# Moving the modulation tiles of a two-layer decoder to other places in the instruction stream

## The chip, the cores and the metric

The kernel runs on one core of one Trainium2 chip. The metric is the device time of one execution in microseconds (us). Three runs of the kernel before gave 2732.73 us as their median (2731.3 to 2734.19).

## The reference

The computation is a trunk of two decoder layers over 1024 tokens of width 1024. A vector `c` modulates each layer: six vectors of 1024 are made from it and used as shift, scale and gate.

```
c_act = silu(c)
for l in range(2):
    mod = c_act @ w_ada[l] + b_ada[l]                 # 6 * 1024 values
    sh1, sc1, g1, sh2, sc2, g2 = split(mod, 6)
    h = rms_norm(x, ln1_g[l]) * (1 + sc1) + sh1
    z = h @ w_in[l]            # pool input, q and kv latents, rope key, two gates
    y_a = pool_mixer(...) @ p_pool[l]
    y_b = causal_attention(...) @ p_attn[l]
    merged = sigmoid(gz_a) * y_a + sigmoid(gz_b) * y_b
    x = x + g1 * (merged @ w_out[l])
    h2 = rms_norm(x, ln2_g[l]) * (1 + sc2) + sh2
    x = x + g2 * (relu(h2 @ w_ff1[l]) ** 2 @ w_ff2[l])
return rms_norm(x, final_g)
```

All arrays are float32. The order of the six vectors matters here: a tile is 128 outputs of `w_ada`, so tiles 0 to 7 of a layer are sh1, 8 to 15 sc1, 16 to 23 g1, 24 to 31 sh2, 32 to 39 sc2 and 40 to 47 g2.

## The kernel before

Every product is made of three matmuls of TensorE on fp32r operands (high times high, high times low, low times high), so that each operand needs a split: a cast on ScalarE (line 305, or 254 for weights) and a subtraction on VectorE (line 306, or 256 for weights; GpSimd makes the latter for a few weights). `x` and `h` are kept transposed, 128 features by 512 tokens a tile, with two token halves `c`.

A layer runs in this order. The latent projections, the pool mixer, and q, k and v with stores to DRAM. Then the gate blocks, a loop `m` from 0 to 7: for `m` under `NA` = 4 a gate block of the input projection (48 matmuls) and the pool projection (24), for the others the pool projection alone; at `m` = 6 `attention_open` (line 1290) takes buffers and loads the first head. Then the attention, a score and a value stage for each head and token half, with the remaining 12 gate blocks (`fill`) as filler on TensorE. Then the attention's projection with the merge, the output projection (8 blocks `m` by two halves, 24 matmuls each; head and tail of three blocks run half by half), in whose tail the second norm of each half is made. Last the channel mixing in eight groups: groups 0 to 6 (`seven`) have an f1 stretch of four blocks (192 matmuls at line 292) and a product stretch (168 matmuls at line 1235, seven products in place of eight), and group 7 is done plainly and makes the next layer's norm.

A modulation tile (`ada_tile`, line 469) is a load of 512 KB into a pair of slots of the buffer `ft`, and one VectorE instruction at line 474 that multiplies it by `cact`, sums along the row and writes one column of `mod`. `ada_pump(n)` takes the next n tiles of the queue `adaq`. The first 16 tiles of layer 0 are made at the start. In the kernel before the other 32 of layer 0 follow in the gate blocks, four in each of the eight `m`, and all 48 of layer 1 in the channel mixing of layer 0: two in the f1 stretch and six in the product stretch of a group, until they are used up at the beginning of group 6. Layer 1 therefore makes no tile in any of its own stages.

Three things order the work. SyncE's queue, which carries all loads, keeps the order in which the program is written; a load waits there until its slots of `ft` are read for the last time, and everything written after it waits behind it. Slots are chosen by `Slots.get`: with `pack` false the pair freed longest ago, with `pack` true (from `attention_open` on, until the merge) one in an already broken quad. The order on the other engines is chosen by the framework's planner at build time, from its own model of times, except in the norm (`norm_tiles`, VectorE) and in a tail of `dense` (TensorE), where it is as written. Three parameters of the vector `mod` are used under names: `g1` and `g2` in `xupd` and `seven`, `sh2` in `norm_x`, and `s2`, made by `scale_vec` from sc2.

Of the kernel before, what the change touches and what calls it, by code (L numbers as in the profile page):

```python
# [19 lines left out]
L = 2  # L20
CH = 512
NC = S // CH
KD = D // P
# [122 lines left out]
NA = 4  # L146
# [18 lines left out]
class Build:  # L165
# [125 lines left out]
    def mm(self, ps, w, x, start, stop):  # L291
        self.nc.tensor.matmul(ps, w, x, start=start, stop=stop)  # L292

    def mm3(self, ps, wh, wl, xh, xl, start, stop):
        self.mm(ps, wh, xh, start, False)
        self.mm(ps, wh, xl, False, False)
        self.mm(ps, wl, xh, False, stop)
# [316 lines left out]
    def start(self, cp):  # L614
# [39 lines left out]
        for k in range(5):  # L654
            self.lo_pool = k >= W_DVE
            self.w_load(True)
            self.w_split(True)
        self.adaq = [(0, j) for j in range(16, 48)]
        self.adaq1 = [(1, j) for j in range(48)]
        s1 = self.scl[:, 0:8]  # L660
        sh1 = self.modc(0, 0)
        for k in range(KD):
# [85 lines left out]
    def layer(self, l):  # L748
# [214 lines left out]
        for m in range(8):  # L963
            if m == 6:
                self.attention_open(l, kk)
            t = F.get(2)
            if m < NA:
                wh, wl = self.w_get("in", l, 9 + m)
                g3 = lambda a: a.rearrange("p (k c) -> p k c", k=KD)
                for c in range(NC):  # L970
                    ps = B.get()
                    self.block_mms(ps.ap, g3(wh), g3(wl), hs, c, range(KD))
                    nc.scalar.activation(t.ap[:, c * CH:(c + 1) * CH], ps.ap, AF.Sigmoid)
                    ps.free()
                self.w_done("in", l, 9 + m)
            wh, wl = self.w_get("pp", l, m // 2)
            vv = lambda a: a.rearrange("p (m k c) -> p m k c", m=2, k=4)[:, m % 2]
            for c in range(NC):
                cs = slice(c * CH, (c + 1) * CH)
                ps = B.get()  # L980
                self.block_mms(ps.ap, vv(wh), vv(wl), (yp, 4), c, range(4))
                if m < NA:
                    nc.vector.tensor_tensor(t.ap[:, cs], ps.ap, t.ap[:, cs], ALU.mult)
                else:
                    nc.scalar.copy(t.ap[:, cs], ps.ap)
                ps.free()
            if m % 2 == 1:
                self.w_done("pp", l, m // 2)
            self.store.dma_start(self.mad[m], t.ap)
            t.free()  # L990
            if l == 0:
                self.ada_pump(4)
        self.drop(yp)

# [9 lines left out]
        mg = {}  # L1004
# [49 lines left out]
        g1 = self.modc(l, 2)  # L1054
        accs = [None] * NC
        xsrc = A["x"] if l == 0 else self.xd

        def xupd(gv, last):
            def ev(m, c, ps):
                cs = slice(c * CH, (c + 1) * CH)  # L1060
                xc = self.x[m, c].ap
                nc.vector.scalar_tensor_tensor(xc, ps.ap, gv[:, m:m + 1], xc, ALU.mult, ALU.add)  # L1062
                if last:
                    if m == 0:
                        accs[c] = F.get(1)
                    self.sq_add(accs[c].ap, xc, m == 0)
            return ev

        for k in range(KD):
            for c, r in enumerate(F.get(2).halves()):  # L1070
                self.x[k, c] = r
                nc.sync.dma_start(self.x[k, c].ap, xsrc[k][:, c * CH:(c + 1) * CH])
        s2 = self.scale_vec(l, 1, self.vec("ln2_g", l * KD, KD))
        sh2 = self.modc(l, 3)

        def post_o(b):
            if isinstance(b, tuple):
                c = b[1]
                self.drop(mg, c)
                self.norm_x(c, accs[c], s2, sh2)  # L1080

        self.h = {}
        self.dense([(("wo", l, m), 0, 1) for m in range(8)], (mg, KD), xupd(g1, True), head=3, tail=3,
                   post=post_o)
        hs = (self.h, KD)


        g2 = self.modc(l, 5)
        F.pack = False
        if l + 1 < L:  # L1090
            self.adaq += self.adaq1

        def ev_f1(hid):
            def ev(m, c, ps):
                hh, hl = self.act(hid, m, c)
                t = F.get(1)
                t2 = F.get(1)
                nc.scalar.activation(t.ap, ps.ap, AF.Relu)
                nc.vector.scalar_tensor_tensor(t2.ap, ps.ap, 0.0, t.ap, ALU.max, ALU.mult)
                nc.scalar.activation(hh, t.ap, AF.Square)  # L1100
                nc.vector.tensor_tensor(hl, t2.ap, hh.bitcast(F32), ALU.subtract)
                t.free()
                t2.free()
            return ev

        for g in range(8):
            if g < NSW:
                self.seven(l, g, hs, g2)
                continue
            self.wlim = len(self.wq)  # L1110
            hid = {}
            self.dense([(("f1", l, 4 * g + m), 0, 1) for m in range(4)], hs, ev_f1(hid),
                       head=3 if g == 0 else 0)
            self.ada_pump(8)
            last = g == 7
            if last:
                self.drop(self.h)
                accs = [None] * NC
                if l + 1 < L:
                    ns = self.scale_vec(l + 1, 0, self.vec("ln1_g", (l + 1) * KD, KD))  # L1120
                    nsh = self.modc(l + 1, 0)

            def post_f(b):
                if last and isinstance(b, tuple):
                    c = b[1]
                    self.drop(hid, c)
                    self.norm_x(c, accs[c], ns, nsh, c == 0)

            f2 = [(("f2", l, g, m // 2), m % 2, 2) for m in range(8)]
            if last and l + 1 == L:  # L1130
                self.dense(f2[:TAIL], (hid, 4), xupd(g2, last))
                self.final_tail(range(TAIL, 8), hid, g2, accs)
            else:
                self.dense(f2, (hid, 4), xupd(g2, last), tail=4 if last else 0, post=post_f)
            self.drop(hid)

    def seven(self, l, g, hs, gv):
# [42 lines left out]
        def load(p):  # L1180
            if p < 4:
                raw[p] = F.get(2)
                nc.sync.dma_start(raw[p].ap, self.A["w_ff2"][l, g, p])
# [30 lines left out]
                    q.free()  # L1214

        def post(b):
            if b < 2:
                self.ada_pump(1)
            if b == 1:
                load(0)  # L1220
            if b == 2:
                load(1)
                prep(0)

        self.dense([(("f1", l, 4 * g + m), 0, 1) for m in F1_ORDER], hs, ev, head=3 if g == 0 else 0,
                   between=(lambda c: (post(1), post(2)) if c == 1 else None) if g == 0 else None, post=post)
        prep(1)

# [11 lines left out]
        for i, (part, p) in enumerate(SEGS):  # L1240
# [18 lines left out]
            else:  # L1259
# [16 lines left out]
                nc.gpsimd.tensor_tensor(x22, x22, u3.ap, ALU.add)  # L1276
                nc.gpsimd.tensor_tensor(x21, x21, u3.ap, ALU.add)  # L1277
                u3.free()
            if i < 6:
                self.ada_pump(1)  # L1280
            if i == 6:
                n = self.wpos["f1", l, 4 * (g + 1)]
                self.wlim = n + 1
# [240 lines left out]
```

## Time and profile before

| what | value |
|---|---|
| time, median of 3 runs | 2732.73 us |
| profiled execution, its time | 2735.55 us |
| profiled execution, its span | 2733.8 us |
| TensorE (PE) busy | 2603.5 us, 95% |
| VectorE (DVE) busy | 1891.6 us, 69% |
| ScalarE (ACT) busy | 1186.2 us, 43% |
| GpSimd (POOL) busy | 832.2 us, 30% |
| mean granted TensorE clock | 0.986 of full speed |

The span is the time from the first to the last instruction of one execution; the rest of its time lies around it. The busy times of the engines overlap, so they don't add up to the span. PEld is the weight load of TensorE, SP the SyncE queue, and a releaser is the instruction whose end let a waiting instruction start.

### The profile page before, as it was taken

Reading aid. Unit: us, or ns where it says so; the run is one execution under the profiler, and the core shown is the slowest. Engines: PE = TensorE matmul, PEld = TensorE weight load, DVE = VectorE, ACT = ScalarE, POOL = GpSimd, SP = SyncE. Lnnn points to the kernel's source line nnn. Section 1 sums busy time; section 2 is a strip of 40 time slices with the busy share of each in tenths; the row PEclk is TensorE's granted clock in tenths of the full one; section 3 lists DMA queues with packets and bytes.
Section 4 is the critical chain, followed back from the end, with each engine's and each line's share of the span. In section 5 each row is a group of like instructions: output and inputs, shape, how many; then the busy total and the mean of one; then the engine's idle time right before and its main releaser. Section 6 shows DMA issues by size and latency. Waiting matters only on the chain.

```text
span 2733.8 us, 31817 instructions
## 1 busy us (share of the span) xinstructions
PE 2603.5 (95%) x11582; PEld 2141.9 (78%) x11582; DVE 1891.6 (69%) x2970; ACT 1186.2 (43%) x2215; POOL 832.2 (30%) x730
## 2 busy tenths in 40 slices
PE   3999879999989999999999999998999999999998
PEld 2788768888868777787888788887787888888887
DVE  8686467776697778777567644875758676676566
ACT  4433156663343333333335334665524343443332
POOL 5010011241054454544310201212303454544430
PEclk9999989999999999999999999999999999999999
DMA  6156555554032223222212624543810111111121
GB/s 232 64 208 237 183 134 128 138 197 169 31 111 71 90 106 124 91 79 84 86 70 82 237 84 120 145 121 103 290 54 16 47 62 62 58 43 39 50 74 62
DMA packets 121229, 299.69 MB, mean 110 GB/s; under 512 B 44016, under 2 KB 46192, under 8 KB 115952
## 3 DMA queue, kind: packets, MB, share of 16 engines
q1 hardware_dynamic: 105584, 236.83, 27.3%
q0 software_dynamic: 13472, 57.68, 5.5%
q10 hardware_dynamic: 2016, 3.15, 0.3%
q8 instruction: 91, 1.49, 0.2%
q14 instruction: 66, 0.54, 0.1%
HBM read 234.70 MB, written 62.91 MB: 109 GB/s over the span
## 4 chain that ended last, share of the span: by engine, by line
PE 72%; DVE 8%; DMA 4%; issue 2%; ACT 1%; POOL 0%; SPq 0%; DVEq 0%; ACTq 0%; POOLq 0%
PE b L292 61%; PE b L1235 11%; DVE rt L306 4%; DVE ft L1246 2%; DMA ft<-in_w_ada_dram 1%; DVE ft L474 1%; DMA ft<-in_w_ff_dram 1%; DMA mad<-ft 0%; DVE ft L1150 0%; DMA rt<-qrd 0%; DVE ft L1422 0%; ACT rt L305 0%; DMA zad<-ft 0%; DVE ft L743 0%; DMA ft<-mad 0%
## 5 line engine op out<-in xcount | busy, mean ns | idle before, releaser
L292 PE MATMUL b<-rt 128*128 128x512 f32 (+5 forms) x9160 | 2046.9, 385 | 73.0 <-ACT rt L305 16.3
L292 PEld LDWEIGHTS b<-rt 128*128 128x128 f32 (+1 forms) x9160 | 1689.2, 190 | 425.5 <-ACT rt L305 17.2
L306 DVE TENSOR_TENSOR rt<-ft,rt 128x256 fp32r<-128x256 f32 (+3 forms) x889 | 611.0, 720 | 164.7 <-ACT rt L305 123.6
L305 ACT CAST rt<-ft 128x512 fp32r<-128x512 f32 (+3 forms) x889 | 420.7, 501 | 483.5 <-POOL ft L1150 86.1
L1235 PE MATMUL b<-rt 128*128 128x512 f32 x2352 | 550.7, 393 | 27.7 <-DVE rt L306 14.7
L1235 PEld LDWEIGHTS b<-rt 128*128 128x128 f32 x2352 | 441.2, 189 | 132.7 <-DVE rt L306 21.6
L256 DVE TENSOR_TENSOR rt<-ft,rt 128x1024 fp32r<-128x1024 f32 (+2 forms) x127 | 160.2, 1265 | 151.8 <-ACT rt L254 148.9
L254 ACT CAST rt<-ft 128x1024 fp32r<-128x1024 f32 (+2 forms) x142 | 145.6, 1035 | 223.1 <-DMA ft<-in_w_ff_dram 122.3
L1246 DVE SCALAR_TENSOR_TENSOR ft<-b,mod,ft 128x512 f32<-128x512 f32 x280 | 204.5, 741 | 24.3 <-PE b L1235 24.3
L1150 POOL TENSOR_TENSOR ft<-ft 128x512 f32<-128x512 f32 x84 | 124.7, 1491 | 252.1 <-DVE ft L1156 184.4
L474 DVE CUSTOM_DVE_ANT_0 ft<-ft,cact,vecs 128x1024 f32<-128x1024 f32 x96 | 147.3, 1545 | 36.5 <-DMA ft<-in_w_ada_dram 36.5
L1156 DVE SCALAR_TENSOR_TENSOR ft<-b,ft 128x512 f32<-128x512 f32 x112 | 76.7, 687 | 84.3 <-ACT ft L1155 83.7
L1198 POOL TENSOR_TENSOR ft<-ft 128x256 f32<-128x256 f32 x56 | 50.3, 898 | 268.7 <-DVE rt L371 115.6
L1267 POOL TENSOR_TENSOR ft<-ft 128x512 f32<-128x512 f32 x56 | 91.5, 1635 | 78.0 <-DVE ft L1246 77.8
L1378 POOL PARTITION_ALL_REDUCE ft<-ft x32 | 64.3, 2009 | 154.4 <-DVE ft L1376 140.4
L1155 ACT ACTIVATE ft<-b 128x512 f32<-128x512 f32 x112 | 66.6, 596 | 102.1 <-PE b L292 101.6
L1423 ACT ACTIVATE ft<-ft 128x512 f32<-128x512 f32 x192 | 92.6, 519 | 36.1 <-DVE ft L1422 36.0
L1422 DVE TENSOR_TENSOR ft<-ft 128x512 f32<-128x512 f32 x192 | 96.8, 563 | 16.3 <-POOL ft L1378 16.3
L1276 POOL TENSOR_TENSOR ft<-ft 128x512 f32<-128x512 f32 x56 | 86.7, 1548 | 35.7 <-ACT ft L1274 35.5
L1208 POOL TENSOR_TENSOR ft<-ft 128x256 f32<-128x256 f32 x56 | 55.9, 999 | 123.6 <-DMA ft<-in_w_ff_dram 73.7
L1277 POOL TENSOR_TENSOR ft<-ft 128x512 f32<-128x512 f32 x56 | 86.9, 1552 | 1.0 <-DVE ft L1246 1.0
L316 ACT ACTIVATE ft<-ft 128x512 f32<-128x512 f32 x67 | 41.5, 630 | 79.7 <-DVE ft L1062 75.4
(153 smaller groups left out, 1515.0 us busy)
## 6 DMA issues: line engine op xcount, KB each, us to landing
ft<-in_w_ff_dram SPq DMA_DIRECT2D x128, 512.0 KB, 3.6
ft<-in_w_ada_dram SPq DMA_DIRECT2D x96, 512.0 KB, 4.5
ft<-in_w_in_dram SPq DMA_DIRECT2D x50, 512.0 KB, 5.5
ft<-in_x_dram SPq DMA_DIRECT2D x32, 256.0 KB, 3.8
qnd<-rt POOLq DMA_DIRECT2D x8, 1024.0 KB, 4.2
kd<-rt POOLq DMA_DIRECT2D x8, 1024.0 KB, 6.6
vd<-rt POOLq DMA_DIRECT2D x16, 512.0 KB, 6.9
mad<-ft POOLq DMA_DIRECT2D x16, 512.0 KB, 3.3
```

The source lines that it names most:

```text
L254: nc.scalar.copy(h[:, :n], raw.ap[:, :n])
L256: eng.tensor_tensor(lo[:, :n], raw.ap[:, :n], h[:, :n].bitcast(F32), ALU.subtract)
L292: self.nc.tensor.matmul(ps, w, x, start=start, stop=stop)
L305: self.nc.scalar.copy(dst_h, src)
L306: self.nc.vector.tensor_tensor(dst_l, src, dst_h.bitcast(F32), ALU.subtract)
L474: nc.vector.tensor_tensor_reduce(out=r.ap, in0=r.ap, in1=self.cact, scale=1.0, scalar=self.vec("b_ada", col), op0=ALU.mult, op1=ALU.add, a ...
L1150: eng.tensor_tensor(out.ap, a.ap, b.ap, ALU.subtract)
L1235: nc.tensor.matmul(ps.ap, a, b, start=start and j + q == 0, stop=stop and j == 1 and q == 2, skip_group_check=True)
L1246: nc.vector.scalar_tensor_tensor(x, ps.ap, v, x, ALU.mult, ALU.add)
L1267: nc.gpsimd.tensor_tensor(x12, x12, u2.ap, ALU.add)
L1422: nc.vector.tensor_tensor(sl, sl, mb.ap[:, off:], ALU.subtract)
L1423: self.last_exp = nc.scalar.activation(sl, sl, AF.Exp, scale=SCALE)
```

## The change

The queue of tiles becomes one list for both layers, and tiles are taken from it in five places, 16 in each. The loop of the gate blocks takes four tiles for each `m` under 4, in both layers. The output projection takes one tile after each of its 16 block halves, in both layers. The channel mixing of layer 0 takes one tile after each of the first three f1 blocks in groups 1 to 5 and one after the first block of group 6; the product stretch takes none. So the layer-0 tiles 16 to 31 fall into its gate blocks and 32 to 47 into its output projection; of layer 1, tiles 0 to 15 fall into the channel mixing of layer 0, 16 to 31 into layer 1's gate blocks and 32 to 47 into its output projection. Because sc2 is now made in the output projection, `s2` is computed just before the first half's norm and no longer ahead of the projection.

```
-        self.adaq = [(0, j) for j in range(16, 48)]
-        self.adaq1 = [(1, j) for j in range(48)]
+        self.adaq = [(0, j) for j in range(16, 48)] + [(1, j) for j in range(48)]
...
             t.free()
-            if l == 0:
+            if m < NA:
                 self.ada_pump(4)
...
-        def xupd(gv, last):
+        def xupd(gv, last, pump=False):
             def ev(m, c, ps):
...
+                if pump:
+                    self.ada_pump(1)
             return ev
...
-        s2 = self.scale_vec(l, 1, self.vec("ln2_g", l * KD, KD))
+        s2 = []
         sh2 = self.modc(l, 3)
 
         def post_o(b):
             if isinstance(b, tuple):
                 c = b[1]
                 self.drop(mg, c)
-                self.norm_x(c, accs[c], s2, sh2)
+                if c == 0:
+                    s2.append(self.scale_vec(l, 1, self.vec("ln2_g", l * KD, KD)))
+                self.norm_x(c, accs[c], s2[0], sh2)
...
-        self.dense([(("wo", l, m), 0, 1) for m in range(8)], (mg, KD), xupd(g1, True), head=3, tail=3,
+        self.dense([(("wo", l, m), 0, 1) for m in range(8)], (mg, KD), xupd(g1, True, True), head=3, tail=3,
                    post=post_o)
...
-        if l + 1 < L:
-            self.adaq += self.adaq1
...
-            self.ada_pump(8)
             last = g == 7
...
         def post(b):
-            if b < 2:
+            if l == 0 and 0 < g < 6 and b < 3:
+                self.ada_pump(1)
+            if l == 0 and g == 6 and b == 0:
                 self.ada_pump(1)
             if b == 1:
                 load(0)
...
-            if i < 6:
-                self.ada_pump(1)
             if i == 6:
```

## Rows read from the trace of the kernel before

**Rows 1.** The page: busy us, share and instructions of an engine; shares of the chain.
```profile
PE 2603.5 (95%) x11582; PEld 2141.9 (78%) x11582; DVE 1891.6 (69%) x2970; ACT 1186.2 (43%) x2215; POOL 832.2 (30%) x730
...
PE 72%; DVE 8%; DMA 4%; issue 2%; ACT 1%; POOL 0%; SPq 0%; DVEq 0%; ACTq 0%; POOLq 0%
```

**Rows 2.** Windows: stretch, length, busy of PE, PEld, DVE, ACT, POOL, clock, DMA.
```profile
133.65:762.23 628.58, 599.00 (x2700) 497.35 (x2698) 436.31 (x751) 299.83 (x574) 104.62 (x94) 0.97 0.49 155
762.23:1327.17 564.94, 540.72 (x2335) 436.42 (x2333) 449.44 (x611) 213.71 (x413) 292.31 (x229) 1.00 0.27 94
1485.51:2095.03 609.52, 594.55 (x2700) 494.93 (x2699) 388.62 (x682) 300.43 (x574) 100.87 (x92) 0.99 0.42 132
2095.03:2630.07 535.04, 531.59 (x2335) 438.83 (x2334) 368.24 (x513) 214.54 (x411) 276.48 (x231) 1.00 0.15 53
```

**Rows 3.** Groups by line: the tile's instruction, busy, mean ns, idle before; its load.
```profile
L474 DVE CUSTOM_DVE_ANT_0 ft<-ft,cact,vecs 128x1024 f32<-128x1024 f32 x96 | 147.3, 1545 | 36.5 <-DMA ft<-in_w_ada_dram 36.5
L474 DVE DVE_READ_ACCUMULATOR2_ANT mod<- 128x1 f32 x96 | 7.7, 80 | 0.0
...
ft<-in_w_ada_dram SPq DMA_DIRECT2D x96, 512.0 KB, 4.5
```

**Rows 4.** Windows around the gate blocks and the attention, columns as in rows 2.
```profile
214.50:300.00 85.50, 84.34 (x371) 69.31 (x370) 58.17 (x85) 26.29 (x41) 4.85 (x8) 1.00 0.60 218
300.00:365.30 65.30, 40.77 (x165) 32.34 (x164) 33.13 (x64) 22.15 (x46) 5.54 (x5) 0.80 0.52 156
530.00:585.00 55.00, 53.48 (x259) 45.10 (x257) 44.90 (x86) 39.87 (x86) 15.04 (x13) 1.00 0.57 173
1569.80:1655.00 85.20, 85.20 (x376) 70.26 (x375) 30.52 (x39) 26.46 (x42) 4.84 (x8) 1.00 0.31 100
1655.00:1710.00 55.00, 55.00 (x264) 46.48 (x263) 30.59 (x67) 29.97 (x62) 10.20 (x10) 1.00 0.39 117
1875.00:1926.00 51.00, 39.97 (x171) 31.94 (x170) 28.28 (x56) 30.20 (x59) 9.45 (x9) 0.87 0.38 134
```

**Rows 5.** Timeline of PE, layer 0's opening of the attention: start, length, what, idle before.
```profile
336.41 4.37 PE L292 MATMUL b<-rt 96*128 96x512 f32 x12 [7.24 <-ACT ft L985]
348.57 1.22 PE L292 MATMUL b<-rt 128*128 128x512 f32 x2 [7.79 <-ACT rt L305]
365.33 5.05 PE L292 MATMUL b<-rt 128*128 128x512 f32 x11 [6.59 <-ACT ft L1391]
```

**Rows 6.** Waits of SyncE's queue from 300 to 366: total us, times, longest.
```profile
SPq L472 <- DVE mod L474: 25.4, 5, 5.9
SPq L472 <- DMA mad<-ft: 16.3, 2, 8.9
```

**Rows 7.** Timeline of POOL at the end of layer 1's attention.
```profile
1895.79 2.38 POOL L256 TENSOR_TENSOR rt<-ft,rt 128x1024 fp32r<-128x1024 f32 x1 [7.43 <-ACT ft L1391]
1903.91 1.80 POOL L1378 PARTITION_ALL_REDUCE ft<-ft  x1 [5.75 <-issue]
```

**Rows 8.** Windows of one group of channel mixing: f1, products; layer 0, then 1.
```profile
988.40:1029.50 41.10, 41.10 (x183) 34.03 (x182) 27.12 (x35) 16.73 (x31) 16.97 (x14) 1.00 0.18 65
1029.50:1074.10 44.60, 41.82 (x181) 33.25 (x180) 40.04 (x57) 15.23 (x32) 27.33 (x21) 1.00 0.38 131
2222.00:2264.50 42.50, 42.50 (x190) 35.17 (x189) 21.14 (x30) 15.52 (x29) 15.47 (x13) 1.00 0.11 38
2264.50:2303.60 39.10, 39.10 (x174) 32.40 (x173) 33.63 (x48) 17.05 (x33) 25.94 (x22) 1.00 0.21 68
```

**Rows 9.** Line 474, ns min/median/max: in 902 to 1290, then in 214 to 300.
```profile
L474 DVE CUSTOM_DVE_ANT_0 ft<-ft,cact,vecs x33: 1268/1753/2321, 907.0 to 1251.7; 128x1024 f32<-128x1024 f32 x33
...
L474 DVE CUSTOM_DVE_ANT_0 ft<-ft,cact,vecs x23: 1274/1282/1286, 225.5 to 292.1; 128x1024 f32<-128x1024 f32 x23
```

**Rows 10.** Windows of layer 0's output projection: its middle, then its tail with norms.
```profile
641.00:709.00 68.00, 67.79 (x299) 55.78 (x299) 30.10 (x39) 18.23 (x24) 0.74 (x1) 1.00 0.22 79
709.00:743.00 34.00, 34.00 (x152) 28.14 (x151) 27.08 (x51) 15.60 (x27) 0.00 (x0) 1.00 0.00 1
```

## The prediction

> **What bounds the kernel now.** I read the page first. TensorE is busy for 2603.5 of 2733.8 us and the chain that ended last runs for 72% through it [rows 1]; the chain's next shares are VectorE 8% and DMA 4%. So time is to be had only where TensorE stands still or runs at its lower clock, and a moved instruction is worth what TensorE waits for it, not its own length.
>
> Then I used what this kernel offers: it does the same layer twice, layer 0 with the moved tiles and layer 1 without any. Two windows per layer with the same number of matmuls show what the tiles cost. The first goes from the rope key to the first product of the channel mixing, the second on to the end of its group 6. The first takes 628.58 us in layer 0 and 609.52 in layer 1, both with 2700 matmuls; the second 564.94 and 535.04, both with 2335 [rows 2]. The differences are 19.06 and 29.90 us, 48.96 together.
>
> Third, where these microseconds lie. In the first window I go by the rate of an undisturbed stretch of the attention, 55.00 us for 264 matmuls or 0.2083 us each [rows 4]. Layer 0's opening of the attention (300 to 365.3) has 165 matmuls in 65.30 us: at that rate 34.4, so 30.9 are lost, with TensorE idle for 24.5 of them and a granted clock of 0.80, a mixture of both levels, since TensorE stood still for up to 7.79 us at a time [rows 4, 5]. Layer 1 has no such loss there. It loses at the other end: 171 matmuls in 51.00 us where 35.6 would do, 15.4 lost, against 1.0 in layer 0 (259 in 55.00) [rows 4]. In the gate blocks before, layer 0 is idle for 1.16 us and layer 1 not at all [rows 4]. 30.9 + 1.0 + 1.2 - 15.4 = 17.7 of the 19.06; the rest is spread.
>
> The opening's cause is seen in SyncE's queue: loads of tiles stood in it for 25.4 us until an earlier tile had been reduced, and for 16.3 us until a stored buffer was free [rows 6], and the loads for the attention are written behind them. These are the tiles of `m` = 6 and 7, written after `pack` has become true, so that one tile gets the slots of the one before.
>
> In the channel mixing the f1 stretch of a group with two tiles is gapless (41.10 of 41.10 us), while the product stretch with six takes 44.60 us, of which VectorE is busy for 40.04; the same stretch of layer 1 takes 39.10, VectorE busy for 33.63 [rows 8]. VectorE is the limit there, and the tiles are what makes it so.
>
> **The change, part by part.**
>
> Channel mixing of layer 0. It loses the 48 tiles and gets 16, in f1 stretches alone. Layer 1's second window is this stage without tiles, hence -29.90 us [rows 2]. What comes back: a third tile in five f1 stretches. VectorE is busy for 27.12 of 41.10 us with two [rows 8]; a third adds at most 2.32 us plus 0.08 for the read-out [rows 3, 9], so 14 us of idle time hide it: 0. Its load is issued ahead of the second w_ff2 load on SyncE, whose first use is some 11 us later, a quarter of the f1 stretch, against 4.5 us to landing [rows 3]. If that cover failed, a tile would cost what one does in the product stretch, 5.50 us / 6 = 0.92 [rows 8], 4.6 for five. Bounds 0 to 4.6; I take 0, since two tiles in the nearest stretch cost nothing.
>
> Gate blocks and attention of layer 0. The 16 tiles of `m` = 4 to 7 leave, eight of them the ones of the opening. The stage becomes layer 1's: -19.06 us [rows 2]. The 16 tiles of `m` = 0 to 3 stay. With 24 tiles in 85.50 us TensorE lost 1.16 us [rows 4], which I leave in: +1.2.
>
> Gate blocks of layer 1: 16 new tiles, at 1.28 + 0.08 us 21.8 us of VectorE [rows 3, 9], where it is busy for 30.52 of 85.20 us [rows 4]. Idle time hides them; the bounds are 0 and layer 0's 1.16 us for more tiles, and I take the upper: +1.2. The attention's loads are written behind them, but by layer 0's window the tiles of four `m` are loaded before `m` = 6 begins.
>
> Output projection, both layers: 16 new tiles in each, 21.8 us of VectorE. From 641 to 709 it is busy for 30.10 of 68.00 us [rows 10], so 37.9 are free and the 13 tiles before the last three want 17.7. SyncE carries 16 more loads among those of the output projection's and f1 weights; the DMA share is 0.22 there [rows 10]. What is queued behind the tiles: the last w_out load behind six of them, one f1 weight behind eight, three behind ten, each needed some 30 us later. The price may come in the tail: from 709 to 743 VectorE has 6.9 us free of 34.00 [rows 10], and the last three tiles want 4.1. If they come just ahead of a norm, f1 waits for it. Below, the bound is 0. Above, it is three tiles that each delay the norm by one reduction and one landing, 3 x (1.4 + 4.5) = 17.7 per layer [rows 3, 9]. Between ends so far apart I go by the nearest row, the tail's free time, which holds the tiles with 2.8 us over and leaves little for a misplaced one: one reduction late, 1.5 us per layer, +3.0. Making `s2` later is one small VectorE instruction and needs the first eight tiles only; it is hidden by the half's remaining blocks.
>
> Sum: -29.90 - 19.06 + 1.2 + 1.2 + 3.0 = -43.6 us. The profiled execution took 2735.55 us, which gives 2692; against the median of the runs, 2732.73, it gives 2689.
>
> **The rivals.**
>
> *The attention's end falls out otherwise.* The 15.4 us at the end of layer 1's attention come from an order on GpSimd: a weight split stands before the last all-reduce, and the all-reduce starts 5.75 us after it with nothing that it waits for [rows 7]; layer 0 has no such stop. The planner may give either order to either layer once the tiles have moved. My sum gives layer 1's order to both. With layer 0's order in one of them 14.4 us more are won (2675), in both 28.8 (2660). For it: layer 0 has it now. Against: layer 0's stage becomes more like layer 1's. The Trainium skill, GPSIMD Engine Reference, section Instruction dispatch, says that the first call of a newly loaded routine on GpSimd pays about 6 us that no instruction shows; the 5.75 us agree. By that rule the stop depends on the order alone, and not on how many tiles there are, so it can come or go with any change that the planner sees.
>
> *The tiles only move their price.* Where VectorE or SyncE is tighter than its busy time tells, the output projection costs the upper bound in both layers and the f1 stretches theirs: -43.6 - 3.0 + 2 x 17.7 + 4.6 = -6.6, or 2726. A half of it, only the opening not healed because another load held it up, gives -43.6 + 19.06 = -24.5, or 2708. For it: the tail's VectorE is 80% busy. Against: its middle is not half busy, GpSimd is nearly idle there, and the tiles run at 1.28 and not 1.75 us [rows 9, 10]. This also covers the case that the change does not do what it says, when the planner lets tiles slip into the products.
>
> *Slower: the chain of the opening is rebuilt in the output projection.* There eight tiles in row, each waiting on SyncE for the reduction of the one before, cost 30.9 us, 3.9 each. If all 32 tiles of the two output projections did so, 125 us would come in for the 49 that go: 2732.73 - 48.96 + 125, about 2809. It is slower from the point at which 13 of the 32 do (49 / 3.9). For it: `x` holds 16 of the 28 slots and weights hold some of the rest, so few pairs are left to the tiles. Against: `pack` is false there, which takes the pair freed longest ago and not the last one, and the blocks between two tiles give 24 matmuls at 42.50 us / 190, or 5.4 us, each [rows 8].
>
> **How the numbers follow.** Forecast 0.52, another end of the attention 0.25, price moved 0.18, slower 0.05. The likeliest gives 2689. For the range I go down to 2662, just short of the first rival's second step, and up to 2713, past the second rival's half way and short of its full price; outside remain the slower case, that full price and a little at the lower end, some 0.2. A change under 0.2% (5.5 us) can't be told from none here. Faster needs new costs under 49 - 5.5 = 43.5 us: all of the first two cases and nearly all of the third, 0.93; within 0.2% 0.03; slower 0.04.
>
> **What would show it.** After the change the two windows of layer 0 should be within 3 us of layer 1's, layer 1's should have grown by no more than 5, the product stretch of layer 0's groups should be 39 us with no tile in it, and TensorE should be gapless from the gate blocks into the attention in both layers at a granted clock of 1.00. Wrong would be gaps of TensorE in the output projection or in the first f1 stretch released by VectorE's norm, loads of tiles that wait on SyncE for tiles, or tiles executed outside their stretches. The POOL order before each layer's last all-reduce decides the first rival.

## The result and the profile after

The changed kernel takes 2659.47 us, the median of four runs (2658.09 to 2661.08), against 2733.19 for the kernel before beside it: a ratio of 0.9735, with a 95% interval of 0.9723 to 0.9747. The prediction said 2689, with a range of 2662 to 2713. So the sign was right, the likeliest case was not, and the time lies 2.5 us below the range. What came is the second step of the first rival, priced at 2660.

The page of the changed kernel answers to [rows 1]: an engine's busy time, the chain's shares, and the group of the tile's instruction from the table of groups (busy, mean ns, idle before).

```profile
PE 2580.6 (97%) x11582; PEld 2136.0 (80%) x11582; DVE 1869.7 (70%) x2970; ACT 1187.3 (45%) x2215; POOL 805.2 (30%) x730
...
PE 90%; DVE 3%; issue 2%; DMA 2%; ACT 1%; POOL 0%; SPq 0%; DVEq 0%; POOLq 0%; ACTq 0%
...
L474 DVE CUSTOM_DVE_ANT_0 ft<-ft,cact,vecs 128x1024 f32<-128x1024 f32 x96 | 128.4, 1346 | 24.9 <-DMA ft<-in_w_ada_dram 24.8
```

TensorE's share of the chain rose from 72 to 90%: the stretches in which TensorE waited for VectorE or a transfer are mostly gone. The 96 tiles are still 96, but one takes 1.35 us on average and no longer 1.55 [rows 3].

The four windows of [rows 2], cut at the same instructions, with the same columns:

```profile
132.98:731.57 598.59, 592.17 (x2700) 493.75 (x2699) 431.78 (x752) 302.34 (x576) 101.51 (x92) 0.99 0.51 163
731.57:1266.32 534.75, 532.60 (x2334) 439.59 (x2333) 388.88 (x545) 210.55 (x411) 270.58 (x230) 0.99 0.20 68
1424.66:2021.22 596.56, 590.82 (x2701) 492.73 (x2700) 432.11 (x747) 300.99 (x574) 101.20 (x92) 1.00 0.51 163
2021.22:2553.72 532.50, 530.03 (x2334) 437.71 (x2333) 368.03 (x512) 215.66 (x411) 273.49 (x231) 1.00 0.16 53
```

They hold the whole gain: 30.0 + 30.2 + 13.0 + 2.5 = 75.7 of the 76.1 us between the profiled executions (2735.55 and 2659.49). Against the prediction's terms:

| window | predicted change | measured | off by |
|---|---|---|---|
| layer 0, rope key to first product | -19.06 + 1.2 + 1.5 = -16.4 | -30.0 | -13.6 |
| layer 0, channel mixing | -29.9 | -30.2 | -0.3 |
| layer 1, rope key to first product | +1.2 + 1.5 = +2.7 | -13.0 | -15.7 |
| layer 1, channel mixing | 0 | -2.5 | -2.5 |

The term of the channel mixing was right to 0.3 us. Both attention windows were off by about the 14.4 us of the first rival. GpSimd's timeline at the end of layer 1's attention answers to [rows 7] (start, length, what, idle before and its releaser):

```profile
1823.98 1.77 POOL L1378 PARTITION_ALL_REDUCE ft<-ft  x1 [3.09 <-DVE ft L1376]
1826.49 0.56 POOL L1392 DMA_DIRECT2D zad<-ft  x1 [0.74 <-ACT ft L1391]
1837.14 2.39 POOL L256 TENSOR_TENSOR rt<-ft,rt 128x1024 fp32r<-128x1024 f32 x1 [10.09 <-DMA ft<-mad]
```

The last all-reduce now stands ahead of the weight split and begins as soon as VectorE's maximum is there. The stop of 5.75 us that ended with "issue" is gone. It was not the whole delay. VectorE's last instructions for that maximum, in the kernel before and in the changed one:

```profile
1888.19 1.34 DVE L1376 TENSOR_TENSOR ft<-ft 128x384 f32<-128x384 f32 x3 [0.44 <-ACT ft L1367]
...
1822.39 1.40 DVE L1376 TENSOR_TENSOR ft<-ft 128x384 f32<-128x384 f32 x3
```

The maximum was complete at 1889.53, and the all-reduce began at 1903.91, 14.4 us later: besides the 5.75 us GpSimd stood for 7.43 us ahead of the weight split [rows 7]. In the changed kernel it begins 0.2 us after it. The windows of the changed kernel around it, first layer 0 (gate blocks; the attention's opening; its end), then layer 1 (gate blocks; the attention's end), answer to [rows 4]:

```profile
214.50:300.00 85.50, 83.44 (x361) 68.30 (x360) 49.10 (x70) 25.58 (x40) 4.84 (x8) 0.98 0.54 186
300.00:360.00 60.00, 60.00 (x286) 50.62 (x285) 33.22 (x71) 32.95 (x67) 11.41 (x11) 1.00 0.45 128
500.00:555.00 55.00, 53.31 (x258) 44.93 (x256) 44.88 (x87) 39.87 (x85) 15.00 (x13) 1.00 0.58 173
1505.00:1590.00 85.00, 84.11 (x370) 69.08 (x369) 49.97 (x71) 26.39 (x42) 4.84 (x8) 1.00 0.57 194
1795.00:1845.00 50.00, 47.82 (x231) 40.31 (x230) 41.19 (x76) 37.12 (x80) 14.40 (x12) 1.00 0.54 166
```

Layer 0's opening is gapless, 60.00 of 60.00 us at a granted clock of 1.00, where it stood still for 24.5 of 65.3. Layer 1's end holds 231 matmuls in 50.00 us, where it held 171 in 51.00. In the gate blocks TensorE is idle for 2.06 us in layer 0, at a granted clock of 0.98, and for 0.89 in layer 1 at 1.00; the prediction charged 1.2 each.

The windows of a group in layer 0's channel mixing (f1 stretch, product stretch; [rows 8]) and of the output projection of layer 0 (middle, tail; [rows 10]):

```profile
775.00:819.00 44.00, 44.00 (x196) 36.45 (x195) 25.04 (x36) 15.43 (x29) 17.24 (x14) 1.00 0.20 72
819.00:857.00 38.00, 38.00 (x170) 31.46 (x169) 34.98 (x48) 16.67 (x33) 24.08 (x20) 1.00 0.20 70
610.00:678.00 68.00, 68.00 (x301) 56.30 (x300) 45.52 (x67) 17.72 (x24) 0.00 (x0) 1.00 0.52 179
678.00:712.00 34.00, 34.00 (x151) 28.14 (x150) 29.57 (x55) 16.25 (x27) 0.00 (x0) 1.00 0.18 62
```

All four are gapless: the third tile in f1 costs nothing, and neither do the tiles of the output projection, where 1.5 us a layer had been charged. The last rival's chain did form. The waits of SyncE's queue in layer 0's output projection and the f1 stretch behind it, 600 to 735 (total us, times, longest):

```profile
SPq L472 <- DVE rt L371: 34.0, 2, 32.4
SPq L472 <- DVE mod L474: 24.8, 8, 9.0
SPq L216 <- DVE mod L474: 12.0, 4, 4.4
```

Loads of tiles and of weights stood behind unread tiles, for 9.0 us at the longest, and one load of a tile stood for 32.4 us until the norm (line 371) had let go of its slots. Nothing that TensorE needed came late by it: TensorE has no gap from 600 to 731.

### The profile page after: what moved, and what is told of

It reads as the page before. It is cut to its first block, busy times and chain, and to the rows that moved or that the text cites. A ratio compares the mean times of both kernels' runs of the same rounds, so it can differ in the third digit from the quotient of the medians.

```text
span 2657.4 us, 31794 instructions
## 1 busy us (share of the span) xinstructions
PE 2580.6 (97%) x11582; PEld 2136.0 (80%) x11582; DVE 1869.7 (70%) x2970; ACT 1187.3 (45%) x2215; POOL 805.2 (30%) x730
## 4 chain that ended last, share of the span: by engine, by line
PE 90%; DVE 3%; issue 2%; DMA 2%; ACT 1%; POOL 0%; SPq 0%; DVEq 0%; POOLq 0%; ACTq 0%
PE b L292 71%; PE b L1237 19%; DVE rt L306 1%; DMA rt<-qrd 1%; DMA vd<-rt 0%; DVE ft L742 0%; ACT rt L254 0%; DMA ft<-od 0%; DMA ft<-zbd 0%; ACT rt L305 0%; POOL vd L902 0%; DMA qrd<-rt 0%; DVE ft L378 0%; DVE ft L1248 0%; POOL ft L854 0%
## 5 line engine op out<-in xcount | busy, mean ns | idle before, releaser
L1237 PE MATMUL b<-rt 128*128 128x512 f32 x2352 | 542.7, 391 | 4.6 <-DVE rt L306 2.6
L1248 DVE SCALAR_TENSOR_TENSOR ft<-b,mod,ft 128x512 f32<-128x512 f32 x280 | 205.2, 741 | 30.2 <-PE b L1237 29.9
L1150 POOL TENSOR_TENSOR ft<-ft 128x512 f32<-128x512 f32 x84 | 125.3, 1500 | 292.1 <-DVE ft L1156 223.7
L474 DVE CUSTOM_DVE_ANT_0 ft<-ft,cact,vecs 128x1024 f32<-128x1024 f32 x96 | 128.4, 1346 | 24.9 <-DMA ft<-in_w_ada_dram 24.8
L1198 POOL TENSOR_TENSOR ft<-ft 128x256 f32<-128x256 f32 x56 | 48.8, 872 | 308.4 <-DVE rt L371 228.6
L1269 POOL TENSOR_TENSOR ft<-ft 128x512 f32<-128x512 f32 x56 | 92.5, 1654 | 90.1 <-DVE ft L1248 63.4
L1278 POOL TENSOR_TENSOR ft<-ft 128x512 f32<-128x512 f32 x56 | 75.2, 1343 | 24.6 <-ACT ft L1276 24.6
L1279 POOL TENSOR_TENSOR ft<-ft 128x512 f32<-128x512 f32 x56 | 76.0, 1356 | 0.0
L1376 DVE TENSOR_TENSOR ft<-ft 128x512 f32<-128x512 f32 (+3 forms) x128 | 64.5, 504 | 16.2 <-ACT ft L1367 9.8
```

What stands on the lines that cost most here:

```text
L474: nc.vector.tensor_tensor_reduce(out=r.ap, in0=r.ap, in1=self.cact, scale=1.0, scalar=self.vec("b_ada", col), op0=ALU.mult, op1=ALU.add, a ...
L1150: eng.tensor_tensor(out.ap, a.ap, b.ap, ALU.subtract)
L1237: nc.tensor.matmul(ps.ap, a, b, start=start and j + q == 0, stop=stop and j == 1 and q == 2, skip_group_check=True)
L1248: nc.vector.scalar_tensor_tensor(x, ps.ap, v, x, ALU.mult, ALU.add)
L1269: nc.gpsimd.tensor_tensor(x12, x12, u2.ap, ALU.add)
```

## Experiments

Experiments 1, 2, 3 and 6 ran on one chip, with runs of the kernel before beside them (median 2733.46 us), and 4, 5, 7 and 8 on another (2732.73). The four windows are those of [rows 2], in that order. They come from one execution of each kernel, which lies up to 6 us from the median of the kernel's runs (experiment 2: 2674.20 against 2668.56), so a difference of 2 or 3 us in one window alone shows little. The last column says whether a weight split stands ahead of the last all-reduce of layer 1 (the stop).

| kernel | median us | ratio, 95% interval | windows, us | stop in layer 1 |
|---|---|---|---|---|
| before | 2732.73 | | 628.6, 564.9, 609.5, 535.0 | yes |
| after | 2659.47 | 0.9735 [0.9723, 0.9747] | 598.6, 534.8, 596.6, 532.5 | no |
| 1 order | 2721.28 | 0.9955 [0.9940, 0.9970] | 625.6, 564.8, 600.3, 535.3 | no |
| 2 toll | 2668.56 | 0.9765 [0.9751, 0.9780] | 601.0, 533.0, 609.4, 532.5 | put back |
| 3 gates | 2704.42 | 0.9891 [0.9874, 0.9908] | 598.9, 564.4, 607.6, 534.7 | yes |
| 4 no tile in layer 1 | 2690.70 | 0.9845 [0.9825, 0.9865] | 597.0, 562.0, 594.4, 535.1 | no |
| 5 mixing | 2695.12 | 0.9857 [0.9839, 0.9876] | 632.9, 534.5, 598.0, 532.6 | no |
| 6 all in f1 | 2720.30 | 0.9950 [0.9935, 0.9965] | 635.8, 558.3, 596.7, 534.5 | no |
| 7 products | 2673.76 | 0.9785 [0.9766, 0.9804] | 599.3, 548.0, 597.4, 532.5 | no |
| 8 late | 2668.98 | 0.9764 [0.9748, 0.9780] | 597.9, 539.1, 597.0, 538.6 | no |

**1. The kernel before with the order alone changed.** The splits that may go to GpSimd at the attention's end are issued behind the last all-reduce; no tile moves.

```
-            nc.gpsimd.partition_all_reduce(mb.ap, m.ap, P, bass_isa.ReduceOp.max)
+            self.last_ar = nc.gpsimd.partition_all_reduce(mb.ap, m.ap, P, bass_isa.ReduceOp.max)
...
-        self.w_pump(self.wpos["pa", l, 0])
+        while self.wl <= self.wlim:
+            self.w_load(True)
+        with self.tc.issue_after(self.last_ar.ins):
+            self.w_pump(self.wpos["pa", l, 0])
```

> The kernel before, with one thing changed: the weight split of the attention's projection may start only after the last all-reduce on GpSimd, which changes the order on GpSimd in layer 1 alone (layer 0 has this order already). Theory A (the stop of 5.75 us on GpSimd between that split and the last all-reduce causes the 15.4 us that layer 1 loses at the attention's end): layer 1's first window falls from 609.5 to about 596 us, the other three windows stay within 1 us, total about 2719 (2716 to 2722). Rival (the order is only a symptom, the end lacks work for TensorE in any order): first window of layer 1 within 3 us of 609.5, total 2730 or more.

Measured: 2721.28 us, 12 below the kernel before. GpSimd at the end of layer 1's attention:

```profile
1887.26 1.78 POOL L1381 PARTITION_ALL_REDUCE ft<-ft  x1 [1.35 <-DVE ft L1379]
...
1897.74 2.39 POOL L256 TENSOR_TENSOR rt<-ft,rt 128x1024 fp32r<-128x1024 f32 x1 [8.71 <-ACT ft L1426]
```

The stop is gone, and layer 1's first window fell by 9.3 us (609.52 to 600.26) with no tile moved in it or near it. So that part of the gain belongs to GpSimd's order and to no tile. Layer 0's first window fell too, by 2.9 us, which I had not expected. Why layer 1's gain is less than the 13.0 of the change was not tried; the profiled execution, at 2724.00 us, was the longest of its four.

**2. The changed kernel with the stop put back.** One ordinary instruction on 16 columns stands on GpSimd ahead of layer 1's last all-reduce. It takes 0.21 us and multiplies by one.

```
+            toll = l == 1 and u == units[-1]
...
+            if toll:
+                nc.gpsimd.tensor_tensor(m.ap[:, :16], m.ap[:, :16], self.ones.bitcast(F32)[:, :16], ALU.mult)
             nc.gpsimd.partition_all_reduce(mb.ap, m.ap, P, bass_isa.ReduceOp.max)
```

> The changed kernel, with one tiny GpSimd multiplication by ones (128x16) put just before the last all-reduce of layer 1, so that GpSimd changes between the two kinds of work once more there. Theory A: the all-reduce starts about 6 us later (0.5 for the instruction, 5.75 for the stop) and layer 1's first window grows from 596.6 by 5 to 10 us, total 2665 to 2670. Rival (the stop is nothing by itself, what cost time in the kernel before was the wait of the weight split for its input): under 2 us, total 2661 or less.

Measured: layer 1's first window grew to 609.41 us, 12.9 more than in the changed kernel, above the 5 to 10 expected, and near the 609.52 of the kernel before. The profiled execution was the longest of its four; by the ratios (0.9765 against 0.9735) the price is 8 us. GpSimd's timeline:

```profile
1831.25 0.21 POOL L1380 TENSOR_TENSOR ft<-ft,ones 128x16 f32<-128x16 f32 x1 [7.70 <-issue]
1837.43 1.80 POOL L1381 PARTITION_ALL_REDUCE ft<-ft  x1 [5.97 <-issue]
```

There are two stops, where I had reckoned with one, and neither waits for anything that the profile shows: 7.70 us ahead of the small instruction and 5.97 ahead of the all-reduce. So GpSimd pays at each change of kind, as it did in the kernel before: 5.75 us ahead of the all-reduce, and 7.43 ahead of the split, which the profile puts down to a ScalarE copy (line 1391) that the split doesn't read [rows 7]. One instruction of 0.21 us undoes most or all of layer 1's gain with every tile in its new place; with experiment 1, where the order alone makes most of that gain, this leaves little of it to the tiles.

**3. Layer 0's gate tiles alone.** Eight tiles for each `m` under 4; the 48 tiles of layer 1 stay in the channel mixing.

```
-            if l == 0:
-                self.ada_pump(4)
+            if l == 0 and m < NA:
+                self.ada_pump(8)
```

> The kernel before, with the 32 tiles of layer 0's gate blocks all in m = 0 to 3, eight in each, and none in m = 4 to 7. Everything else as before; by the planner's list layer 1 keeps its order on GpSimd. Theory C (the opening is late because of the tiles written after the attention's buffers are taken, at m = 6 and 7): layer 0's first window falls from 628.6 to 596 to 602, layer 1's stays at 609.5, total 2703 to 2708. Rival (32 tiles are too many ahead of the attention's loads on SyncE, wherever they stand): layer 0's first window above 615, total above 2718.

Measured: layer 0's first window 598.91 us, the 598.59 of the changed kernel, though all 32 tiles are in the gate blocks. The second is as before. Layer 1 kept the wrong order and its window (607.55):

```profile
1866.02 2.38 POOL L256 TENSOR_TENSOR rt<-ft,rt 128x1024 fp32r<-128x1024 f32 x1 [7.07 <-ACT ft L1391]
1874.43 1.80 POOL L1378 PARTITION_ALL_REDUCE ft<-ft  x1 [6.02 <-issue]
```

So what heals the opening is that no tile stands in `m` = 4 to 7, and it is worth 29.7 us, not the 19.06 of the difference between the layers. Whether it takes the tiles of `m` = 6 and 7 alone, those that the prediction blamed, was not tried. Layer 0 already had the good order, and keeps it.

**4. Layer 0's attention as changed, no tile in layer 1's stages.** The 48 tiles of layer 1 are in the channel mixing as in the kernel before.

```
-            if m < NA:
+            if l == 0 and m < NA:
                 self.ada_pump(4)
...
-            if l == 0 and 0 < g < 6 and b < 3:
-                self.ada_pump(1)
-            if l == 0 and g == 6 and b == 0:
+            if b < 2:
                 self.ada_pump(1)
...
+            if i < 6:
+                self.ada_pump(1)
```

> The other part alone: layer 0's tiles as in the changed kernel (16 in the gate blocks, 16 in its output projection), layer 1's 48 in layer 0's channel mixing as before, so that layer 1 has none in its own stages. If the parts are independent: layer 0's first window 598 to 601, its second 563 to 566, and layer 1's first 596 to 600, since the planner's list shows the other order on GpSimd here too although nothing is changed in layer 1. Total about 2733 - 30 - 13 = 2690 (2686 to 2694). Rival (the order's gain in layer 1 belongs to the tiles placed there): 607 to 610 in layer 1's first window, total 2703.

Measured: 596.96 us for layer 0's first window, and 561.96 for its channel mixing, which keeps its loss. Layer 1's first window is 594.40: the order there turned good though nothing in that layer was changed. All three lie 1 to 2 us below what I had expected; the profiled execution, at 2685.86 us, was the shortest of its four.

```profile
1850.19 1.77 POOL L1381 PARTITION_ALL_REDUCE ft<-ft  x1 [3.09 <-DVE ft L1379]
...
1863.58 2.44 POOL L256 TENSOR_TENSOR rt<-ft,rt 128x1024 fp32r<-128x1024 f32 x1 [10.32 <-ACT rt L305]
```

It also prices layer 1's 32 new tiles. Without them and without the stop the window is 594.40 here and 596.71 in experiment 6; with them it is 596.56 to 597.96 (after, 5, 7, 8). They cost 0 to 3.6 us, no more than single executions differ by; 2.7 had been charged.

**5. The channel mixing and layer 1 as changed, layer 0 as before.** All 32 tiles of layer 0 return to the eight `m`, none is in its output projection.

```
-            if m < NA:
+            if l == 0 or m < NA:
                 self.ada_pump(4)
...
-        ... xupd(g1, True, True), head=3, tail=3,
+        ... xupd(g1, True, l == 1), head=3, tail=3,
```

> One part of the change alone: layer 1's tiles as in the changed kernel (16 in layer 0's channel mixing, 16 in layer 1's gate blocks, 16 in its output projection), layer 0's 32 in its eight gate blocks as before. If the parts are independent: layer 0's first window as before (626 to 630), its second as after (533 to 536), and, since the planner's list shows the other order on GpSimd at the end of layer 1's attention, layer 1's first window 596 to 598. Total about 2733 - 30 - 13 - 2 = 2688 (2684 to 2692). Rival (the 32 new tiles in layer 1 cost time that another gain hid in the changed kernel): layer 1's first window above 600.

Measured: 2695.12 us. Layer 0's channel mixing fell to 534.46 us (-30.5) and layer 1's first window to 597.96, while layer 0's attention kept its loss, with 4.3 us more than in the kernel before (632.89, where 630 at most was expected); these 4.3 us are most of the 7 by which the time lies above the expected 2688, and why they came was not tried. Neither part needs the other for its gain: the channel mixing falls here, and layer 0's attention falls in experiment 4.

**6. The kernel before with all 48 tiles in the f1 stretches.** Two after each f1 block, eight in a group, and none issued in the products.

```
-            if b < 2:
-                self.ada_pump(1)
+            self.ada_pump(2)
...
-            if i < 6:
-                self.ada_pump(1)
```

> The kernel before, with the 48 tiles of layer 1 all in the f1 stretches of layer 0's channel mixing (two after each f1 block, so eight a group), none in the product stretches; the gate blocks of layer 0 keep their 32. Theory B (it matters where a tile stands, not how many there are: the product stretch has no VectorE time left, the f1 stretch has): layer 0's second window falls from 564.9 to 535 to 540. Rival (it is the number of tiles in the stage: VectorE or the loads are short over the whole group): 550 to 565. In both cases layer 0's first window stays at 628 or 629, and the planner's list for this kernel has the other order on GpSimd at the end of layer 1's attention, which by theory A gives 596 for layer 1's first window. Theories A and B together: 2688 to 2697.

Measured: 2720.30 us, where 2688 to 2697 was expected, and all of that gain is the order in layer 1, which turned good here too (-12.8 in its first window). Layer 0's channel mixing is 6.7 us shorter, where tiles that f1 hides would have given 30, and the window ahead of it, which ends with the f1 stretch of group 0, 7.2 longer: nothing is gained. The cause that I had named, that VectorE is full in the products and has room in f1, is not all of it. The product stretch of one group, 1032.65 to 1075.70, then SyncE's waits from 985 to 1075:

```profile
1032.65:1075.70 43.05, 40.11 (x175) 32.24 (x173) 37.57 (x52) 17.75 (x36) 28.49 (x24) 1.00 0.23 74
```

```profile
SPq L472 <- DVE rt L306: 27.5, 3, 14.9
...
SPq L1183 <- DVE mod L474: 7.5, 2, 6.1
```

The loads of tiles waited 27.5 us for slots, and the loads of w_ff2 (line 1183), which are written behind them, up to 6.1 us for a tile to be reduced; one tile ran at 1042, in the products. With eight tiles in an f1 stretch the loads run late. How the loss divides between a late w_ff2 and VectorE's late work was not taken apart. The change puts three there, and they are free.

**7. The changed kernel with the three tiles in the products.** Same number in each group, only the stretch is another.

```
-            if l == 0 and 0 < g < 6 and b < 3:
-                self.ada_pump(1)
-            if l == 0 and g == 6 and b == 0:
-                self.ada_pump(1)
...
+            if l == 0 and (i < 3 and 0 < g < 6 or g == 6 and i == 0):
+                self.ada_pump(1)
```

> The changed kernel, with the three tiles of groups 1 to 5 of layer 0's channel mixing in the product stretch and not in the f1 stretch. Theory D (the product stretch has no VectorE time for a tile: six cost 4.1 us a group in the kernel before, 0.7 each): 2 us a group more, 10 in all, layer 0's second window 543 to 547, total 2668 to 2672. Theory E (a group has room for a few tiles wherever they stand, and only the six or eight of the earlier kernels were too many): second window 533 to 537, total within 3 us of the changed kernel's 2659.

Measured: 2673.76 us, and 548.01 us for the window, 13.3 more than in the changed kernel for 16 tiles (group 6's one moves too), 0.83 each. [Rows 8] had given 0.92, and both values lie just above the ranges expected. TensorE's timeline in one product stretch, then its waits in the whole window, the two largest of four:

```profile
929.72 6.66 PE L1233 MATMUL b<-rt 128*128 128x512 f32 x28 [0.72 <-DVE rt L306]
937.09 4.36 PE L1233 MATMUL b<-rt 128*128 128x512 f32 x18 [0.71 <-DVE ft L1244]
```

```profile
PE b L1233 <- DVE ft L1244: 5.5, 5, 2.6
PE b L1233 <- DVE rt L306: 4.4, 7, 0.8
```

Of TensorE's 11.9 us of waiting 9.9 end with VectorE, as they should if it is the limit there; the other 2.0 end with ScalarE. In the changed kernel it waits for 2.1 us in all.

**8. The changed kernel with the output projection's tiles later.** Two after each block of the second half in place of one after every block, so the last ones stand further into the tail.

```
-                if pump:
-                    self.ada_pump(1)
+                if pump and c == 1:
+                    self.ada_pump(2)
```

> The changed kernel, with the 16 tiles of each output projection written after its second half's blocks alone, two after each, so that six in place of three are written among the two norms of the tail. By the forecast's price for a tile that comes ahead of a norm (one reduction of 1.4 us, at most 5.9 us with its landing): the tail has 4.4 us of VectorE left in the changed kernel, three more tiles want 4.1, so 0 to 6 us a layer, total 2660 to 2671. Rival (the tail is full): over 6 us a layer, total above 2671. If nothing changes (within 2 us of 2659), the tail never was the place that could have cost something.

Measured: 2668.98 us; by the ratios (0.9764 against 0.9735) 8 us more than the changed kernel. The tail itself didn't grow: the first windows, which contain it, are 597.89 and 597.01 us. The second ones grew by 4.4 and 6.1. Layer 0's two windows, and the first microseconds of the products of group 0 in layer 0 and in layer 1:

```profile
132.90:730.79 597.89, 590.87 (x2700) 492.50 (x2698) 425.65 (x746) 298.21 (x570) 97.54 (x89) 1.00 0.51 163
730.79:1269.92 539.13, 535.64 (x2334) 439.44 (x2333) 392.61 (x551) 212.76 (x417) 272.87 (x233) 0.99 0.20 68
...
733.00:750.00 17.00, 13.51 (x36) 7.49 (x36) 16.87 (x20) 8.00 (x16) 11.62 (x10) 0.76 0.00 0
2028.00:2048.00 20.00, 17.34 (x50) 10.63 (x48) 18.81 (x25) 7.84 (x16) 12.25 (x13) 0.74 0.16 45
```

Against the changed kernel, six VectorE instructions and six of ScalarE have slipped from the first window into the second (752 to 746 and 545 to 551; 576 to 570 and 411 to 417): VectorE comes to the products behind its work. There it is busy for 16.87 of 17.00 us, and 18.81 of 20.00 in layer 1; TensorE stands still in between, and the granted clock is 0.76 and 0.74, between the two levels. The changed kernel in stretches of the same length, as far behind the first product:

```profile
733.78:750.78 17.00, 14.85 (x50) 10.72 (x50) 17.00 (x26) 8.32 (x20) 12.47 (x13) 0.80 0.18 62
2023.95:2043.95 20.00, 17.53 (x74) 13.19 (x72) 20.00 (x31) 10.70 (x26) 15.37 (x16) 1.00 0.15 53
```

VectorE is full there in both kernels, so its share alone doesn't tell them apart. TensorE does: 50 and 74 matmuls in the changed kernel, 36 and 50 with the later tiles. So the tail has as little room as the prediction feared, but the bill comes behind it, in the first products; the change's own places stay short of it.

## Why the prediction was wrong

**What bounds the kernel, and where the time lies:** right. The four windows hold 75.7 of 76.1 us, and the two causes named in layer 0 (the opening, the products) were cured by their own edits (experiments 3 and 5).

**Channel mixing, -29.90:** right, -30.2. The reason given, VectorE full in the products, holds at 0.83 us a tile (experiment 7); that f1 hides tiles holds for three and not for eight (experiment 6).

**Gate blocks and attention of layer 0, -19.06:** this is the step that failed, in the sentence "My sum gives layer 1's order to both". The difference between the layers had two parts of opposite sign: 30.9 us lost in layer 0's opening, and 15.4 lost at the end of layer 1's attention. To equate "layer 0 without its tiles" with layer 1 as it stood meant that layer 0 would take over layer 1's own fault when its tiles moved. It didn't: the loss of the opening went by itself (experiment 3: 29.7 us) and the good order stayed. The sum should have taken the 30.9 less what the gate tiles cost.

**Layer 1 unchanged but for +2.7:** the same failure from the other side. Its order turned good, which is worth 9.3 us where it is forced (experiment 1) and 8 to 13 where it is taken away again (experiment 2); 14.4 had been priced. By the runs the wrong order was the rare one: of the nine kernels in the table in which nothing forces it (all but experiment 1) it stands in layer 1 only in the kernel before and in experiment 3. The trace of before could not tell that, but it showed each order once. To leave each layer its own order, the first rival's first step, would have needed less of an assumption than to give the wrong one to both. The sign that the prediction named for this, GpSimd's order before the last all-reduce, did decide it.

**Gates and output projection, +5.4:** about the right size: 0 to 3.6 us in layer 1 against 2.7, with the idle time in the gate blocks (2.06 and 0.89) and none in the output projection of layer 0, where 1.5 had been charged. The mechanisms feared there exist (SyncE's waits of 24.8 us; VectorE's 16.87 of 17.00 us in experiment 8) but don't reach TensorE in this arrangement. At the first products of layer 0, where VectorE is full, it stands still for 2.1 us in the changed kernel; in layer 1 of the kernel before, which has no tiles, it stood still for 3.4 at that place.

**The range:** it ended at 2662, "just short of the first rival's second step". That step was then what happened. A case that the text itself priced at 2660 lay 2 us outside a range that was to hold all but 2 in 10. That it agrees with 2659.47 to 1 us is in part luck: by windows that rival gives -30.8, -29.9, -11.7 and 0, or 72.4 together, where the profiled executions show 75.7 in these windows, and the medians 73.3 in all.

**Left open:** why layer 1's channel mixing fell by 2.5 us. It is 532.5 in all kernels with one tile after every block of layer 1's output projection (after, 2, 5, 7) and 534.5 to 535.3 in those without tiles there (before, 1, 3, 4, 6). A part of it lies in the first 20 us of the products of group 0, in the kernel before and in the changed one:

```profile
2095.03:2115.03 20.00, 16.93 (x67) 13.27 (x65) 19.97 (x28) 8.61 (x19) 13.82 (x13) 0.91 0.17 53
2021.22:2041.22 20.00, 17.53 (x73) 13.20 (x72) 20.00 (x30) 9.76 (x23) 14.25 (x14) 1.00 0.15 53
```

TensorE makes 73 matmuls there and no longer 67; why VectorE, full in both, keeps it waiting less was not tried. Open too is what in the planner's model tips GpSimd's order: it turned in experiment 4 with no edit in layer 1.

## What to carry to other kernels

Two repetitions of a stage, one with the suspected work and one without, give its price only after each has been searched for losses of its own: take the loss that the edit removes from the place where it lies, and don't net it against a fault of the other copy. Where a planner orders an engine, an order seen in one of two copies is not a property of the stage: price both orders and let the range hold both. Work put into another stage's idle time is free up to what its load queue and buffers carry, so spread it thinly: three tiles in a stretch cost nothing, eight gave back all of the gain.

## What the runs showed of the hardware

GpSimd's stop between an ordinary elementwise instruction and an all-reduce comes in both directions: in experiment 2 it stood idle for 7.70 us before a 0.21 us instruction that followed an all-reduce, and for 5.97 us before the all-reduce that followed that. The Trainium skill, GPSIMD Engine Reference, section Instruction dispatch, puts about 6 us on the first call of a newly loaded routine; the second stop agrees, and the first shows that the way back to ordinary instructions is paid too. GpSimd's queue has a pair of `MODIFY_POOL_CONFIG` at both changes. In experiment 2 one stands ahead of the small instruction (line 1380) at 1823.6 us, and the last one of the all-reduces (line 1381) at 1831.7. In the changed kernel the all-reduces (line 1378) have their last at 1607.6, and none at the end of layer 1's attention:

```profile
L1380 POOLq MODIFY_POOL_CONFIG  x2: 37/37/37, 1823.6 to 1823.7; - x2
L1381 POOLq MODIFY_POOL_CONFIG  x6: 3/37/42, 319.9 to 1831.7; - x6
...
L1378 POOLq MODIFY_POOL_CONFIG  x4: 37/40/42, 317.0 to 1607.6; - x4
```

In the changed kernel the way back stands ahead of the weight split, in 10.09 us of idle time. The profile puts these down to a transfer of `mad`, which the split doesn't read; in experiments 4 to 8 the same idle time is 10.06 to 10.53 us and is put down to ScalarE's line 305. How much of it is the stop itself was not tried; no instruction is shown to wait for that split.

A tile and GpSimd slow each other where they meet, as far as a comparison of places shows it; no run changed this alone. In the gate blocks a tile takes 1.28 us [rows 9]. In the channel mixing of the kernel before its median was 1.75 and the longest 2.32; at such a place GpSimd's instructions, of the kind that elsewhere takes 1.29, were long too. Before, VectorE and then GpSimd:

```profile
993.07 2.32 DVE L474 CUSTOM_DVE_ANT_0 ft<-ft,cact,vecs 128x1024 f32<-128x1024 f32 x1
```

```profile
992.14 2.16 POOL L1276 TENSOR_TENSOR ft<-ft 128x512 f32<-128x512 f32 x1 [3.19 <-ACT ft L1274]
994.26 2.27 POOL L1277 TENSOR_TENSOR ft<-ft 128x512 f32<-128x512 f32 x1
```

In the changed kernel all 16 tiles of that stage take 1.27 to 1.29 us (line 474 from 731 to 1270); in one group they run from 865.65 to 871.2, while GpSimd does nothing from 862.3 to 871.3. The Trainium skill, SBUF — State Buffer, section Who interferes with whom, says that a VectorE instruction with two inputs in SBUF contends with a GpSimd instruction that reads SBUF; the 2.32 and 1.28 us agree. The tiles' lower mean, 1.35 us against 1.55, goes with this.
